# Convolutions taken from a queue of their own, first transposes in other PSUM banks, and norms placed elsewhere in a hybrid decoder layer

## The chip, the cores and the metric

The kernel runs on one core of a Trainium2 chip. The metric is the device time of one execution in microseconds (us). The core's engines are PE (TensorE, matrix products into PSUM), DVE (VectorE), ACT (ScalarE), POOL (GpSimd) and SP (SyncE, which here issues DMAs); each runs its own list of instructions in order and waits on semaphores for the others.

## The reference, cut to what matters

One layer is computed for 512 prompt tokens and 8 x 4 sample tokens, 544 in all, with 1024 channels, in fp32. An RMSNorm stands before and after each of three blocks:

```python
x = x + 0.5 * rmsnorm(swiglu(rmsnorm(x, n_ffn1_pre), ffn1_wg, ffn1_wu, ffn1_wd), n_ffn1_post)   # 1024 -> 2816 -> 1024
mix, new = mixer(rmsnorm(x, n_mix_pre), ...)
x = x + rmsnorm(mix, n_mix_post)
x = x + 0.5 * rmsnorm(swiglu(rmsnorm(x, n_ffn2_pre), ffn2_wg, ffn2_wu, ffn2_wd), n_ffn2_post)

def swiglu(x, wg, wu, wd):
    return (silu(x @ wg) * (x @ wu)) @ wd

def mixer(u, ...):
    rg_x, rg_g, z, xbc, dt_raw, g_rg, g_ssd = split(u @ w_in)          # 1024 -> 10272
    rg_xc = causal_conv(rg_x, rg_conv_w, rg_conv_b)                     # 4 taps along time
    h = rg_lru(rg_xc, ...)       # gates sigmoid(rg_xc @ wa + ba), sigmoid(rg_xc @ wx + bx), then a scan over time
    y_rg = h * gelu(rg_g)
    xs, Bs, Cs = split(silu(causal_conv(xbc, ssd_conv_w, ssd_conv_b)))
    y = ssd_scan(xs, softplus(dt_raw + bias), -exp(a_log), Bs, Cs, ...)  # 32 heads in 8 groups, chunks of 128 tokens
    y = (y + ssd_d * xs) * silu(z)
    y_ssd = y * rsqrt(mean over each group(y * y) + EPS) * ssd_norm_w
    m = sigmoid(g_rg) * (y_rg @ w_proj_rg) + sigmoid(g_ssd) * (y_ssd @ w_proj_ssd)
    return m @ w_out, new states
```

## The kernel before, in words

Activations lie with channels on the partitions and the 544 tokens along the free axis, in two halves of 272 (`HALF`). Weights come in blocks of up to 1024 x 128. ACT casts a block to a rounded part `wh` (L75), and DVE subtracts that from the block, which gives the rest `wl` (L79); `WRAW` = 2 raw loads and `WBLK` = 4 split blocks are held. Activations are split in the same way (`xh`, `xl`). A block's product is three passes for each of its eight 128 x 128 tiles, wh on xh, wh on xl and wl on xh, summed in PSUM: `gemm` (L285) for both halves of the tokens, `gemm_half` (L317) for one half, where `pair` puts two blocks side by side in one accumulator.

PSUM has three kinds of tile: `acc` (two of two banks each), `ps` (two of one bank), `py` (one of two banks).

PE's order is the order in which the code is written. The lists of the other engines are put in order by a scheduler, from dependencies and priorities (`urgent()` raises one; weight splits are lowered); edges without a semaphore ("NOSYNC") fix an order on one engine.

Beside the gemms runs background work, written as generators in the list `bg`: norms, transposes, the RG-LRU (`rg_steps`, eight channel tiles taken in pairs, r0 = 0, 2, 4, 6), dt (`dt_steps`), the convolutions of the SSD branch and its groups (`group_steps`). `ptick()` counts gemm matmuls; at each `pace`-th, `tick()` lets the first generator of the list go on to its next `yield`. `wait(n)` is n yields. What a generator writes to PE thus stands at a place counted in gemm matmuls.

The places that the change touches, in the order of the program:

- *Start.* x is transposed untouched (L565, `to_half`): x[0], x[1] and x2a give the first 272 tokens, eight chunks of 128 channels into eight banks of all three kinds. ACT makes xh (L570), DVE xl (L571, `evac_half`). Squares for the norm (L546) run beside; the norm's factor `fac` reaches the first products later (L606, `first_factors`). The first gemm's accumulator takes the place of the `acc` tile that holds chunks 0 and 5. The other 272 tokens are squared, scaled (`scaled`) and transposed in the background (`first_norm`).
- *First transposes of x itself.* `turn_steps` (L655, DVE copies L656) brings x into the transposed layout for the residual; a step is five transposes.
- *RG pair 6* is the last pair; its gates are matmuls into `py` (L937), a sigmoid after each (L939), two gates for each of two channel tiles.
- *SSD groups.* For each of 8 groups the main stream has units for B, C, x0, x1 (their products are evacuated into `cb`, L734 to L737, and the last columns into `cq`, L877), gates, and z. A convolution is a first tap on ACT (L863), three taps on DVE (L865), a tanh on ACT (L1009), and two products on DVE (L1010, L1011). Then `group_steps`: `A(c)` transposes B and x of chunk c (L1041, L1043), scales on DVE (L1046) and takes exponentials on ACT (L1048, L1062); `Bs(c)` is the chunk's products; s0 to s4 are the sample tokens'. `s2(p)` evacuates two state transposes with an ACT copy each (hT, L1168). In `bg` the four convolutions of a group stand as entries of their own ahead of its `group_steps`, each with a `wait(3)` behind it.
- *Norms between blocks.* `between(..., waits)` waits so many ticks before its sums, factors and transposes.
- *End.* `y_units` adds the last product pair of a half to y (L439) and squares it (L426); in the last half `turn.last` weighs y by the norm's weight (L1470), `turn_last` transposes it (L1474, L1558), `finish` sums squares over channels with matmuls into one column per 128 tokens (L1536, three sources, 18 matmuls), takes the factor (L236, L239, L240 to L243) and adds it to x (L1553).

Of the kernel before, what the change touches and what calls it, by code (L numbers as in the profile page):

```python
# [18 lines left out]
P = 128  # L19
D = 1024  # L20
KD = 8
# [13 lines left out]
class Weights:  # L35
# [30 lines left out]
    def _split_next(self):  # L66
# [26 lines left out]
WARM = 10  # L93

# [5 lines left out]
def hybrid_layer_kernel(  # L100
# [159 lines left out]
    pace = [8]  # L260
# [4 lines left out]

    def tick():
# [29 lines left out]
    def pair(kt, rh, rl, h, keep=None, key=None):  # L296
# [17 lines left out]
    def gemm_half(acc, j, wb, kt, rh, rl, h):  # L314
        for k in range(kt):
            for i, (w, r) in enumerate(((wb[0], rh), (wb[0], rl), (wb[1], rh))):
                PE.matmul(acc[:, j, :TH], w[:, k, :], r[k][:, HALF[h]],  # L317
                          start=(k == 0 and i == 0), stop=(k == kt - 1 and i == 2))
                ptick()
# [22 lines left out]
    def ffn(hid, open_pool, post, late=None, turn=None):  # L342
# [30 lines left out]
        for kind, i, h in ffn_order():  # L373
            if kind == "gu":
# [13 lines left out]
                else:  # L388
                    kept = keep if i == 1 else None
                    acc = pair(KD, xh, xl, h, kept, "g")  # L390
# [14 lines left out]
    def y_units(pool, tag, kt, rh, rl, n2, h, sqa, add, qscale, keep, turn=None):  # L405
# [6 lines left out]
        else:  # L412
            acc = pair(kt, rh, rl, h, keep if n2 in KEPT else None, n2)
            first, last = ((0, 3), (SECOND[0], SECOND[3]))[h]
            step = 1 if n2 == last else 2
            alone = turn is not None and n2 == last
            if alone:
                qv = turn.squares()
            else:
                q = pool.tile([P, T], F32, tag=tag, name="sq", bufs=6 if tag == "ld" else 2)  # L420
                qv = two(q)
            for j in range(0, 2, step):
                yv = yb[:, 2 * n2 + j:2 * n2 + j + step, HALF[h]]
                with urgent():
                    evac_y(yv, acc[:, j:j + step, :TH], add)
                    S.activation(qv[:, j:j + step], yv, AF.Square, scale=qscale)  # L426
                    if alone:
                        turn.last(j)
                    elif n2 == first:
                        V.tensor_add(sqa[:, HALF[h]], q[:, HALF[0]], q[:, HALF[1]])  # L430
                    else:
                        for i in range(j, j + step):
                            V.tensor_add(sqa[:, HALF[h]], sqa[:, HALF[h]], q[:, HALF[i]])
            if turn is not None and not alone:
                turn.pair(n2)

    def evac_y(y, acc, add):
        if add:
            V.tensor_add(y, y, acc)  # L439
        else:  # L440
            S.copy(y, acc)

# [92 lines left out]
    def factors(srcs, on_vector=()):  # L535
# [1065 lines left out]
```

## Time and profile before

| | |
|---|---|
| three runs | 1747.27, 1741.66, 1745.37 us, median 1745.37 |
| the profiled execution | 1746.04 us, span 1744.2 us (1.8 us lie around the span) |
| PE busy | 1692.1 us, 97% of the span |
| DVE, ACT, POOL busy | 1000.7, 739.6, 260.4 us |
| matmuls of the gemms in three passes, one of them (L285, wh on xh) | 2576, mean 292 ns with overlap |
| bytes | 206.21 MB in 205551 packets, mean 118 GB/s |

How to read it: the span is what the trace covers, from the first to the last recorded instruction; the profiled execution's own time lies 1.8 us above it. Matmuls overlap in the array, so the mean of 292 ns is longer than the pitch from one to the next. Busy times say what an engine did, not whether the end waited for it: for that one reads the waits.

### The profile page before, as it was taken

Reading aid. Unit: us, or ns where it says so; the run is one execution under the profiler, and the core shown is the slowest. Engines: PE = TensorE matmul, PEld = TensorE weight load, DVE = VectorE, ACT = ScalarE, POOL = GpSimd, SP = SyncE. Lnnn points to the kernel's source line nnn. Section 1 sums busy time; section 2 is a strip of 40 time slices with the busy share of each in tenths; the row PEclk is TensorE's granted clock in tenths of the full one; section 3 lists DMA queues with packets and bytes.
Section 4 is the critical chain, followed back from the end, with each engine's and each line's share of the span. In section 5 each row is a group of like instructions: output and inputs, shape, how many; then the busy total and the mean of one; then the engine's idle time right before and its main releaser. Section 6 shows DMA issues by size and latency. Waiting matters only on the chain. (4 is left out here: it accounts for less than half of the span.)

```text
span 1744.2 us, 32098 instructions
## 1 busy us (share of the span) xinstructions
PE 1692.1 (97%) x13485; PEld 1649.7 (95%) x13485; DVE 1000.7 (57%) x1764; ACT 739.6 (42%) x1204; POOL 260.4 (15%) x376
## 2 busy tenths in 40 slices
PE   8999999999999998999999999999999999999997
PEld 8899999999999997998988988999999999999997
DVE  5632333237757578788689687776558332233335
ACT  6323221234568674545545545434246423221233
POOL 0000000000222125345344333230000000000000
PEclk9999999999999998999999999999999999999999
DMA  6223232233543333524443535666324323223231
GB/s 208 84 75 114 74 98 84 87 97 109 164 156 112 101 97 107 165 88 113 146 144 93 157 114 155 214 189 221 137 80 139 115 68 109 85 85 97 75 120 52
DMA packets 205551, 206.21 MB, mean 118 GB/s; under 512 B 10461, under 2 KB 191785, under 8 KB 205150
## 3 DMA queue, kind: packets, MB, share of 16 engines
q1 hardware_dynamic: 196588, 178.49, 33.1%
q0 software_dynamic: 8336, 24.54, 4.3%
q8 instruction: 106, 1.74, 0.4%
q10 hardware_dynamic: 482, 1.12, 0.2%
q14 instruction: 39, 0.32, 0.1%
HBM read 178.43 MB, written 25.69 MB: 117 GB/s over the span
## 5 line engine op out<-in xcount | busy, mean ns | idle before, releaser
L75 ACT CAST wh<-wraw 128x1024 fp32r<-128x1024 f32 (+1 forms) x274 | 283.6, 1037 | 645.9 <-PE acc L285 535.0
L285 PE MATMUL acc<-xh,wh 128*128 128x272 f32 x2576 | 544.3, 292 | 0.1
L285 PE MATMUL acc<-xh,wl 128*128 128x272 f32 x2576 | 541.7, 292 | 0.0
L285 PE MATMUL acc<-xl,wh 128*128 128x272 f32 x2576 | 539.3, 291 | 0.0
L79 DVE TENSOR_TENSOR wl<-wraw,wh 128x1024 fp32r<-128x1024 f32 (+1 forms) x274 | 331.3, 1212 | 320.3 <-ACT wh L75 317.2
L285 PEld LDWEIGHTS acc<-xh,wh 128*128 128x128 f32 x2576 | 409.0, 190 | 3.5 <-issue 1.4
L285 PEld LDWEIGHTS acc<-xh,wl 128*128 128x128 f32 x2576 | 407.3, 190 | 2.6 <-issue 1.2
L285 PEld LDWEIGHTS acc<-xl,wh 128*128 128x128 f32 x2576 | 408.3, 190 | 1.2 <-issue 0.4
L317 PE MATMUL acc<-xh,wh 128*128 128x272 f32 x384 | 114.6, 298 | 3.3 <-DVE xl L571 3.3
L317 PE MATMUL acc<-xh,wl 128*128 128x272 f32 x384 | 113.8, 296 | 0.0
L317 PE MATMUL acc<-xl,wh 128*128 128x272 f32 x384 | 113.4, 295 | 0.0
L386 DVE TENSOR_TENSOR gate<-gate,acc 128x544 f32<-128x544 f32 x36 | 26.0, 721 | 132.0 <-PE acc L285 132.0
L865 DVE SCALAR_TENSOR_TENSOR cv<-cb,hp,cv 128x568 f32<-128x568 f32 x96 | 93.9, 978 | 1.1
L285 PE MATMUL acc<-hh,wh 128*128 128x272 f32 x448 | 92.5, 288 | 0.0
L285 PE MATMUL acc<-hl,wh 128*128 128x272 f32 x448 | 92.2, 287 | 0.0
L285 PE MATMUL acc<-hh,wl 128*128 128x272 f32 x448 | 92.2, 288 | 0.0
L1551 POOL TENSOR_TENSOR xtok<-xtok,yo 32x512 f32<-32x512 f32 x1 | 1.3, 1257 | 535.7 <-ACT yo L1550 535.7
L725 POOL MEMSET cb<- 128x3 f32 x40 | 4.1, 102 | 510.1 <-PE acc L317 434.7
L317 PEld LDWEIGHTS acc<-xh,wh 128*128 128x128 f32 x384 | 74.4, 194 | 3.9 <-DVE xl L571 3.4
L317 PE MATMUL acc<-hh,wh 128*128 128x272 f32 x256 | 75.0, 293 | 0.0
L317 PEld LDWEIGHTS acc<-xl,wh 128*128 128x128 f32 x384 | 74.4, 194 | 0.5
L317 PEld LDWEIGHTS acc<-xh,wl 128*128 128x128 f32 x384 | 74.2, 193 | 0.3
(397 smaller groups left out, 2642.5 us busy)
## 6 DMA issues: line engine op xcount, KB each, us to landing
wraw<-in_w_in_dram SPq DMA_DIRECT2D x34, 1024.0 KB, 5.6
wraw<-in_ffn_wu_dram SPq DMA_DIRECT2D x24, 1024.0 KB, 5.3
wraw<-in_ffn_wg_dram SPq DMA_DIRECT2D x23, 1024.0 KB, 5.2
wraw<-in_ffn_wd_dram SPq DMA_DIRECT2D x20, 1024.0 KB, 5.2
wraw<-in_w_in_dram SPq DMA_DIRECT2D x18, 512.0 KB, 4.3
big<-acs_dram SPq DMA_DIRECT2D x32, 256.0 KB, 5.6
big<-in_state_ssd_dram SPq DMA_DIRECT2D x32, 256.0 KB, 6.0
out_dram<-big POOLq DMA_DIRECT2D x32, 256.0 KB, 3.6
```

The lines of the kernel that those rows point to most:

```text
L75: c = nc.scalar.copy(h[:, :kt], src)
L79: nc.vector.tensor_sub(l[:, :kt], src, h[:, :kt].bitcast(F32))
L285: PE.matmul(acc[:, h, :TH], w[:, k, :], r[k][:, HALF[h]], start=(k == 0 and i == 0), stop=(k == kt - 1 and i == 2))
L317: PE.matmul(acc[:, j, :TH], w[:, k, :], r[k][:, HALF[h]], start=(k == 0 and i == 0), stop=(k == kt - 1 and i == 2))
L386: V.tensor_mul(two(gs[j]), two(gs[j]), acc[:, :, :TH])
L725: G.memset(buf[:, 0:3], 0.0)
L865: V.scalar_tensor_tensor(o[:, :CO], buf[:, k:k + CO], ws[k], o[:, :CO], op0=ALU.mult, op1=ALU.add)
L1551: G.tensor_add(x[:n, cs], x[:n, cs], o[:n])
```

## The change

What it does, in the order of the program:

1. The first transposes go to the banks in the order acc, acc, acc, acc, ps, ps, py, py (two chunks to a tile). The first gemm of all (`apart`) does its sixteen passes with wh first, then its eight with wl. The cast of block 0 now stands behind chunk 2's xh, that of blocks 1 to 3 behind the last chunk's. `factors` is divided: `squares` after the evacuations (x2a's square on ACT behind the last xh), `factors` for Ln and Exp.
2. `pace` starts at 6, not 8.
3. The convolutions of the SSD groups go to a list `convs`. `conv_next(g, limit)` takes one if it belongs to group g, fewer than `limit` of that group have been taken, and at least `APART` = 7 ticks have passed since the last. It is called in each tick of the *previous* group's steps (limit 2, from A(3) on 3, from Bs(2) on 4), for group 0 in the ticks of RG pair 6 (limit 2). What is left is taken at the start of the group itself, with `wait(3)` behind each.
4. `between` waits 12 for 10 ticks in FFN 1 (first half) and 13 for 11 between mixer and FFN 2.
5. In the last pair of each half, y's part j = 0 is evacuated, squared and summed as soon as its own 24 matmuls are done (`done`), not after both.
6. At the end j = 0's squares are added to `sqa` on DVE; its sums run ahead, and only the last part's squares (`ql`, three matmuls) are summed after the last product; the two are added on DVE.

The core of the diff:

```diff
-        if self.after is not None and 0 < self.n_blk < WBLK:
-            after = self.after if self.n_blk == 1 else self.after2
-            self.tc.add_manual_dep(c.ins, after.ins.name, NOSYNC, reason="the input comes first")
+        if self.n_blk < WBLK:
+            self.tc.add_manual_dep(c.ins, self.after[self.n_blk > 0].ins.name, NOSYNC, reason="the input comes first")
...
-    pace = [8]
+    pace = [6]
...
+    def conv_take():
+        g, work = convs.pop(0)
+        work()
+        convs_done[g] += 1
+        conv_at[0] = ticks[0]
+
+    def conv_next(g, limit):
+
+        if convs and convs[0][0] == g and convs_done[g] < limit and ticks[0] >= conv_at[0] + APART:
+            conv_take()
+
     def tick():
+        ticks[0] += 1
         while bg:
             try:
                 next(bg[0])
                 return
             except StopIteration:
                 bg.pop(0)
+        if convs:
+            conv_next(convs[0][0], 4)
```

The queue's two users (the generator of RG pair 6 and a group's steps; every other `wait` in the two became `steps` in the same way):

```diff
+        def steps(n):
+            for _ in range(n):
+                yield
+                if r0 == KD - 2:
+                    conv_next(0, 2)
+
...
-            yield from wait(4)
+            yield from steps(4)
...
     def group_steps(g, tiles):
+        while convs_done[g] < 4:
+            conv_take()
+            yield from wait(3)
         Bt, Ct, x0, x1, z0, z1 = (tiles[i] for i in range(6))
+        limit = [2]
+
+        def steps(n):
+            for _ in range(n):
+                yield
+                conv_next(g + 1, limit[0])
+
...
+        yield from steps(2)
         A(3)
-        yield from wait(3)
+        limit[0] = 3
+        yield from steps(3)
         yield from s3(0)
         Bs(2)
-        yield from wait(3)
+        limit[0] = 4
+        yield from steps(3)
         yield from s2(1)
         yield from s3(1)
         Bs(3)
...
-            bg.append(conv_steps(f, buf, out, i))
+            convs.append((g, lambda f=f, buf=buf, out=out, i=i: conv_ssd(f, buf, out, i)))
```

The start:

```diff
+    def squares(srcs, on_vector=(), after=()):
 
         m = len(srcs)
-        ssq, t, r = (pi.tile([P, m], F32, name=f"{n}{m}", tag=n, bufs=2) for n in ("ssq", "ssq_t", "ssq_r"))
+        ssq = pi.tile([P, m], F32, name=f"ssq{m}", tag="ssq", bufs=2)
...
+                if i in after:
+                    put_behind(a, W.after[1])
+        return xn, ssq
+
+    def factors(ssq):
+
+        t, r = (pi.tile(list(ssq.shape), F32, name=f"{n}{ssq.shape[1]}", tag=n, bufs=2) for n in ("ssq_t", "ssq_r"))
+        rstd_act(ssq, t, r, W.after[1])
+        return r
...
     first = ((xt[0], P), (xt[1], P), (x2a, 16))
-
-    a, b, t = acc_tile(), acc_tile(), py_tile()
-    banks = [a[:, 0], b[:, 0], ps_tile(), ps_tile(), t[:, 0], a[:, 1], b[:, 1], t[:, 1]]
+    banks = []
+    for t in (acc_tile(), acc_tile()):
+        banks += [t[:, 0, :], t[:, 1, :]]
+    banks += [ps_tile(), ps_tile()]
+    t = py_tile()
+    banks += [t[:, 0, :], t[:, 1, :]]
...
-    first_r = factors(first, (1,))[1]
-    turned = None
+    turned = []
     for k in range(KD):
-        a = evac_half(banks[k][:, :TH], 0, k)
-        if turned is not None:
-            tc.add_manual_dep(a.ins, turned.ins.name, NOSYNC, reason="in the order of their use")
-        turned = a
-        if k == 3:
-            W.after = a
-    W.after2 = turned
+        turned.append(evac_half(banks[k][:, :TH], 0, k))
+        if k:
+            put_behind(turned[k], turned[k - 1])
+    W.after = [turned[2], turned[-1]]
+    first_ssq = squares(first, (1,), (2,))[1]
```

Order of the passes, last pairs and end:

```diff
-            gemm_half(acc, j, wbs[j], kt, rh, rl, h)
+            gemm_half(acc, j, wbs[j], kt, rh, rl, h, apart and j == 0)
+            if done is not None:
+                done(acc, j)
...
+    def gemm_half(acc, j, wb, kt, rh, rl, h, apart=False):
+
+        passes = ((0, rh), (0, rl), (1, rh))
+        order = [(k, p) for k in range(kt) for p in passes]
+        if apart:
+            order = [(k, p) for k in range(kt) for p in passes[:2]] + [(k, passes[2]) for k in range(kt)]
+        for n, (k, (w, r)) in enumerate(order):
+            PE.matmul(acc[:, j, :TH], wb[w][:, k, :], r[k][:, HALF[h]], start=(n == 0), stop=(n == len(order) - 1))
+            ptick()
...
+            def out(acc, j, step=1):
                 yv = yb[:, 2 * n2 + j:2 * n2 + j + step, HALF[h]]
                 with urgent():
                     evac_y(yv, acc[:, j:j + step, :TH], add)
-                    S.activation(qv[:, j:j + step], yv, AF.Square, scale=qscale)
+                    S.activation(ql if alone and j else two(q)[:, j:j + step], yv[:, 0] if alone and j else yv,
+                                 AF.Square, scale=qscale)
                     if alone:
                         turn.last(j)
+                    if alone and j:
+                        pass
                     elif n2 == first:
                         V.tensor_add(sqa[:, HALF[h]], q[:, HALF[0]], q[:, HALF[1]])
                     else:
                         for i in range(j, j + step):
                             V.tensor_add(sqa[:, HALF[h]], sqa[:, HALF[h]], q[:, HALF[i]])
+
+            acc = pair(kt, rh, rl, h, keep if n2 in KEPT else None, n2, out if n2 == last else None)
+            if n2 != last:
+                out(acc, 0, 2)
             if turn is not None and not alone:
                 turn.pair(n2)
 
```

```diff
-        yield from between(f1.tmp, xT, sqa, R_F1POST, R_MPRE, h, table, ((4, 10, 1), (4, 8, 1))[h])
+        yield from between(f1.tmp, xT, sqa, R_F1POST, R_MPRE, h, table, ((4, 12, 1), (4, 8, 1))[h])
...
-            bg.append(between(tmp, xT, sqa, R_MPOST, R_F2PRE, h, table, ((1, 11, 0), (4, 8, 1))[h]))
+            bg.append(between(tmp, xT, sqa, R_MPOST, R_F2PRE, h, table, ((1, 13, 0), (4, 8, 1))[h]))
...
+        V.memset(v[:, :, :3], 1.0)
         turn_last(2 * SECOND[3], 0)
-        for i, t in enumerate(TAIL):
-            for m, (src, o) in enumerate(srcs(t)):
-                PE.matmul(v[:NT[t], 0, i:i + 1], src[:, o:o + NT[t]], ones_d[:, 0:1], start=(m == 0), stop=(m == 2))
-        turn_last(2 * SECOND[3] + 1, 1)
+        for m, src in enumerate((sqa[:, 2 * P:], turn.q)):
+            if m:
+                sm = f2.pool.tile([P, 3], F32, name="fm")
+                S.copy(sm, v[:, 0, :3])
+                turn_last(2 * SECOND[3] + 1, 1)
+            for i, t in enumerate(TAIL):
+                PE.matmul(v[:NT[t], m, i:i + 1], src[:, P * i:P * i + NT[t]], ones_d[:, 0:1], start=True, stop=True)
         ra, r = (f2.pool.tile([P, 3], F32, tag=n, name=n) for n in ("fa", "fr"))
         with urgent():
-            rstd_act(v[:, 0, :3], ra, r, table)
+            V.tensor_add(sm, sm, v[:, 1, :3])
+            rstd_act(sm, ra, r, table)
```

Where the change moves instructions, the lists of an engine show it (line, operation, result <- sources, shape; "x2" is two of it in a row). Line numbers of the changed kernel are higher. First ACT at the start, before; L570 is a chunk's xh, L546 a square, L75 a block's cast (the first one shown is block 1's):

```order
L570 ACTIVATE xh_101<-acc,w1T 128x272
L75 CAST wh<-wraw 128x1024
L570 ACTIVATE xh_102<-py,w1T 128x272
L546 ACTIVATE xn,ssq_378<-yb 128x1024 x2
L546 ACTIVATE xn,ssq_378<-xs_in 32x1024
L75 CAST wh<-wraw 128x1024
L236 ACTIVATE ssq_t_379<-ssq_378,eps_t 128x3
L75 CAST wh<-wraw 128x1024
```

and after, where L608 is xh, L578 a square, L237 and L240 Ln and Exp:

```order
L608 ACTIVATE xh_101<-py,w1T 128x272
L608 ACTIVATE xh_102<-py,w1T 128x272
L578 ACTIVATE xn,ssq_249<-x2a 16x1024
L578 ACTIVATE xn,ssq_356<-yb 128x1024
L237 ACTIVATE ssq_t_295<-ssq_249,eps_t 128x3
L578 ACTIVATE xn,ssq_356<-yb 128x1024
L240 ACTIVATE ssq_r_296<-ssq_t_295 128x3
L578 ACTIVATE xn,ssq_356<-xs_in 32x1024
L75 CAST wh<-wraw 128x1024
L237 ACTIVATE ssq_t_364<-ssq_356,eps_t 128x3
L75 CAST wh<-wraw 128x1024
```

Block 1's cast, which stood between chunks 6 and 7, now follows four squares, Ln and Exp; block 0's (not shown) stands behind chunk 2.

PE in the first products of FFN 1, before, where the second of the gate's products ends and its stream of background steps runs out (L317 a pass of the gemm, L655 a step of `turn_steps`):

```order
L317 MATMUL acc<-xh_102,wh 128x272
L317 MATMUL acc<-xl_110,wh 128x272
L317 MATMUL acc<-xh_102,wl 128x272
L655 MATMUL ps<-ident,yb 128x128 x4
L655 MATMUL ps<-ident,xs_in 128x32
L655 MATMUL ps<-ident,yb 128x128 x4
L655 MATMUL ps<-ident,xs_in 128x32
L655 MATMUL ps<-ident,yb 128x128 x4
L655 MATMUL ps<-ident,xs_in 128x32
```

and after, a little earlier in the stream (L344 the pass, L693 the step):

```order
L693 MATMUL ps<-ident,yb 128x128 x4
L693 MATMUL ps<-ident,xs_in 128x32
L344 MATMUL acc<-xh_97,wh 128x272
L344 MATMUL acc<-xl_105,wh 128x272
L344 MATMUL acc<-xh_97,wl 128x272
L344 MATMUL acc<-xh_98,wh 128x272
L344 MATMUL acc<-xl_106,wh 128x272
L344 MATMUL acc<-xh_98,wl 128x272
L693 MATMUL ps<-ident,yb 128x128 x4
L693 MATMUL ps<-ident,xs_in 128x32
```

Of eight steps five stood in a row after matmul 192; now each has six matmuls behind it.

ACT in the gates of RG pair 6, before (L939 a gate's sigmoid, L1009 the tanh of a convolution of group 0, L734 to L737 and L877 evacuations, L863 a convolution's first tap):

```order
L939 ACT_TABLE_LOAD
L939 ACTIVATE in<-py,pT 128x568
L1009 ACTIVATE cv<-cv 128x568
L939 ACTIVATE in<-py,pT 128x568
L734 COPY cb<-acc 128x272
L736 COPY cb<-acc 128x240
L737 COPY cb<-acc 128x8x4
L75 CAST wh<-wraw 128x1024
L877 COPY cq<-cb 128x27
L863 ACTIVATE cv<-cb,hp 128x568
L939 ACTIVATE in<-py,pT 128x568 x2
```

and after (L983 the sigmoid, L1053 the tanh):

```order
L1053 ACT_TABLE_LOAD
L1053 ACTIVATE cv<-cv 128x568
L983 ACT_TABLE_LOAD
L983 ACTIVATE in<-py,pT 128x568 x2
L772 COPY cb<-acc 128x272
L774 COPY cb<-acc 128x240
L775 COPY cb<-acc 128x8x4
L75 CAST wh<-wraw 128x1024
L915 COPY cq<-cb 128x27
L901 ACTIVATE cv<-cb,hp 128x568
L1053 ACTIVATE cv<-cv 128x568
L983 ACTIVATE in<-py,pT 128x568 x2
```

Conv 0's tanh moved from behind the first sigmoid to ahead of it, with a table load of its own; conv 1's tanh, which came after the pair's square roots, now stands ahead of the third sigmoid.

More of the change, by code (lines that the diff above doesn't have):

```diff
@@ L389, in ffn @@
                     kept = keep if i == 1 else None
-                    acc = pair(KD, xh, xl, h, kept, "g")
+                    acc = pair(KD, xh, xl, h, kept, "g", apart=late is not None and (i, h) == (0, 0))
                     g = silu(acc, late() if late and h == 0 else None)
@@ L546, in factors @@
                 a = S.activation(xn[i][:n], x[:n], AF.Square, scale=D ** -0.5, accum_out=ssq[:n, i:i + 1])
-                if W.after is not None:
-                    tc.add_manual_dep(a.ins, W.after2.ins.name, NOSYNC, reason="the first half comes first")
-        rstd_act(ssq, t, r, table)
-        return xn, r
+                if i in after:
[5 more added lines that the diff above has]
+        return r
     def scaled(srcs, engines):
-        xn, r = factors(srcs)
+        xn, ssq = squares(srcs, after=(0, 1, 2))
+        r = factors(ssq)
         for i, (x, n) in enumerate(srcs):
@@ L941, in rg_steps @@
                 lst.append(g)
-                yield from wait(4)
+                yield from steps(4)
             G.tensor_mul(gxs[j][:, :CO], gxs[j][:, :CO], xcs[j][:, :CO])
@@ L952, in rg_steps @@
             avs.append(av)
-        yield from wait(4)
+        yield from steps(4)
         ths = []
@@ L962, in rg_steps @@
             V.scalar_tensor_tensor(gx, t, 1.0, gx, op0=ALU.add, op1=ALU.mult)
-        yield from wait(4)
+        yield from steps(4)
         rc = slice(LP + 2, LP + 2 + 7 * NB - 6, 7)
@@ L968, in rg_steps @@
             V.tensor_mul(gxs[j][:, :CO], gxs[j][:, :CO], gas[j][:, :CO])
-        yield from wait(4)
+        yield from steps(4)
         for j, r in enumerate(rs):
@@ L985, in rg_steps @@
             ahead["z"] -= 1
-            yield from wait(4)
+            yield from steps(4)
     def rg_final():
@@ L1184, in s3 @@
                 V.tensor_copy(st8["yos"][:, p], yo[:, :P])
-            yield from wait(3)
+            yield from steps(3)
             for i in range(2):
@@ L1195, in s3 @@
                 dma(o_s_ssd[0, 4 * i:4 * i + 4, hs].rearrange("b h d n -> (h d) b n"), h0[i])
-                yield from wait(3)
+                yield from steps(3)
         def s4():
@@ L1241, in group_steps @@
         s4()
-        yield from wait(3)
+        yield from steps(3)
         ys = []
@@ L1258, in group_steps @@
         fin()
-        yield from wait(12)
+        yield from steps(12)
         v = py_tile()
@@ L1265, in group_steps @@
             last_tanh[0] = rstd_act(v[:, :, :TH], two(sqs[0]), two(r))
-        yield from wait(3)
+        yield from steps(3)
         for p in range(2):
@@ L1270, in group_steps @@
             dma(ys_dram[f], ys[p])
-        yield from wait(3)
+        yield from steps(3)
     last_tanh = [None]
```

59 lines of the change are left out of this document (25 added, 34 removed).

## The prediction

> **What bounds the kernel now.** I read the page first (engine totals), then the granted clock by window, then TensorE's waits, then timelines of the places where the diff reaches. On the page:
>
> ```profile
> PE 1692.1 (97%) x13485; PEld 1649.7 (95%) x13485; DVE 1000.7 (57%) x1764; ACT 739.6 (42%) x1204; POOL 260.4 (15%) x376
> ```
>
> TensorE is busy for 1692.1 of 1744.2 us, and the change removes only some tiny matmuls, so what it can win is idle time of TensorE and time at a lowered clock. The windows (columns: length, busy time of PE, PEld, DVE, ACT, POOL, granted clock, DMA share, GB/s) show where both are:
>
> ```profile
> core 0: us, PE busy (x) PEld busy (x) DVE busy (x) ACT busy (x) POOL busy (x), PEclk, DMA share, GB/s
> 10.00:20.00 10.00, 6.74 (x32) 6.44 (x32) 8.15 (x22) 9.36 (x19) 0.00 (x0) 0.66 0.81 265
> 50.00:60.00 10.00, 7.51 (x35) 6.10 (x36) 9.11 (x23) 3.04 (x7) 0.00 (x0) 0.69 0.00 1
> 620.00:630.00 10.00, 7.83 (x50) 7.61 (x49) 6.37 (x10) 4.87 (x10) 2.16 (x6) 0.83 0.16 59
> 630.00:640.00 10.00, 10.00 (x82) 10.00 (x81) 5.08 (x9) 8.19 (x14) 2.82 (x4) 1.00 0.21 55
> 660.00:670.00 10.00, 4.56 (x21) 4.37 (x21) 6.78 (x18) 2.97 (x6) 4.26 (x10) 0.57 0.64 197
> 676.00:1160.00 484.00, 466.03 (x3915) 440.41 (x3914) 390.12 (x791) 239.25 (x451) 189.74 (x253) 0.99 0.46 136
> ...
> 1345.00:1720.00 375.00, 374.26 (x2989) 373.26 (x2988) 136.33 (x172) 113.66 (x154) 0.00 (x0) 1.00 0.28 90
> ```
>
> Full speed is 82 matmuls in 10 us (630 to 640), 0.122 us each. From 10 to 20 and 50 to 60 only 32 and 35 were done, from 660 to 670 only 21. From 1345 to 1720 TensorE hardly idles: nothing to win there. Its largest waits by releaser (total, times, longest):
>
> ```profile
> PE ps L1041 <- ACT big L1168: 8.0, 5, 2.2
> PE ps L1043 <- DVE in L1010: 7.0, 2, 5.2
> PE ps L1165 <- ACT small L1059: 4.0, 3, 2.6
> PE acc L317 <- DVE xl L571: 3.3, 1, 3.3
> PE ps L655 <- DVE xT L656: 2.6, 4, 0.8
> ```
>
> **The start.** The first gemm waits for the bank of its accumulator, which a transpose also used:
>
> ```profile
> 10.51 0.23 PE L565 MATMUL py<-ident,x2a 16*128 16x16 f32 x1
> 14.00 0.60 PE L317 MATMUL acc<-xh,wh 128*128 128x272 f32 x1 [3.26 <-DVE xl L571]
> 22.67 0.93 PE L606 MATMUL ps<-dg,ones_d 128*128 128x128 f32 x6
> 9.39 0.29 ACT L236 ACTIVATE ssq_t<-ssq,eps_t 128x3 f32<-128x3 f32 x1
> 9.72 0.20 ACT L239 ACTIVATE ssq_r<-ssq_t 128x3 f32<-128x3 f32 x1
> 12.73 1.04 ACT L75 CAST wh<-wraw 128x1024 fp32r<-128x1024 f32 x1
> 14.05 1.06 ACT L546 ACTIVATE xn<-yb 128x1024 f32<-128x1024 f32 x1
> 13.46 0.90 DVE L571 SCALAR_TENSOR_TENSOR xl<-acc,w1T,xh 128x272 fp32r<-128x272 f32 x2
> 15.21 1.21 DVE L79 TENSOR_TENSOR wl<-wraw,wh 128x1024 fp32r<-128x1024 f32 x1
> ```
>
> With the new banks the first accumulator is freed by the first chunks, and the gemm can begin when the transposes end, 10.51 + 0.23, about 10.8. Its sixteen wh passes then go at the pace of DVE's xl (0.45 each, with one wl of 1.21 between): by these rows the last xl is ready near 13.4, the passes end near 13.7, and eight wl passes end near 14.7. But block 1 is now late. Before, its cast began at 12.73, ahead of all squares but the first two. After, the order on ACT puts x2a's square, three more squares (1.06 each), Ln and Exp (0.29, 0.20) ahead of it: xh ends near 12.2, plus 4 x 1.06 + 0.49 is about 16.9, cast to 17.9, wl to 19.2. So TensorE, idle from 14.7, gets two passes in near 18 and goes on at 19.2, most likely at a lowered clock again (0.66 in this window before). Gemm 48 with the L606 transposes ended at 22.67 + 0.93 = 23.6; I get 24.3: **+0.7**. Ends: -2.5 (the squares yield, only the first wait goes) and +2.5 (the lowered clock lasts on over another 3.4 us).
>
> **The first background transposes.** At pace 8 they end in a burst of five:
>
> ```profile
> L655 PE MATMUL ps<-ident,yb 128*128 128x128 f32 x20 | 4.0, 332 | 2.6 <-DVE xT L656 2.6
> ```
>
> The burst idles 2.6 us on DVE's copies out of two banks, and the clock falls: the mean of 0.69 from 50 to 60 is 6.2 us at half speed (2 x 0.31 x 10). Less about 0.8 of idle in it, half of that is lost: 2.7. At pace 6 the same steps stand six gemms (0.73 us) apart and all end before the pass does; DVE is not behind. **-5.3** (-2.6 if only the idle goes; -6.5). The Trainium skill (TensorE: Matmul & The Clock Gate, HAM oscillation) gives the rule "no PE-idle gaps >~3.4µs": single idles of 0.8 would then cost no clock, this term would be -2.6 and the sum 2.7 less. The clock of 0.69 in that row, with no idle longer than 0.8, is against it here.
>
> **The RG gates of pair 6.** There the new queue puts conv 0 and conv 1 of group 0 between the gates, and ACT's order changes: conv 0's tanh now stands ahead of sigmoid 1, conv 1's tanh ahead of sigmoid 3.
>
> ```profile
> 620.85 1.28 ACT L939 ACT_TABLE_LOAD   x1
> 624.62 0.73 ACT L939 ACTIVATE in<-py,pT 128x568 f32<-128x568 f32 x1 [2.48 <-PE py L937]
> 626.50 0.68 ACT L1009 ACTIVATE cv<-cv 128x568 f32<-128x568 f32 x1 [1.15 <-DVE cv L865]
> 634.25 0.73 ACT L939 ACTIVATE in<-py,pT 128x568 f32<-128x568 f32 x1 [1.78 <-PE py L937]
> 624.77 1.63 DVE L865 SCALAR_TENSOR_TENSOR cv<-cb,hp,cv 128x568 f32<-128x568 f32 x2
> 627.68 0.94 PE L937 MATMUL py<-big,small 128*128 128x284 f32 x6
> 665.77 0.69 PE L1043 MATMUL ps<-ident,in 128*128 128x128 f32 x2 [5.16 <-DVE in L1010]
> 650.53 0.67 DVE L1010 SCALAR_TENSOR_TENSOR in<-cv 128x512 f32<-128x512 f32 x1
> ```
>
> The tanh can't start before the convolution ends on DVE (624.77 + 1.63 = 626.4); it ends at 627.2, a second table load (1.28) follows, and sigmoid 1 ends at 629.2 instead of 625.35. It holds py, the one bank, so gate matmuls 2 wait from 627.7 to 629.3 (1.6). Conv 1's tanh comes at best near 636.4 (its evacuations, a cast and its first tap are queued behind sigmoid 2), so sigmoid 3 ends near 637.8 and gates 4 wait about 3.1. Sigmoid 4 ends near 639.6, not 634.98. The chain through Exp, Sqrt and scans to x1 thus starts some 5 us later, but the stretch of DVE between it and x1 has less in it: conv 1's output (650.53, 0.67 + 0.15) is done earlier, one wl and three scalings come after x1: about -1.5. TensorE arrives at x1's transposes 4.7 us plus some clock later, so its 5.16 there is mostly the same wait, taken earlier; x1, before at 665.77, comes near 669.4. **+3.6**, from 0 (the delay fits into the 5.16) to +6. The Trainium skill (ScalarE: Activation LUTs, What ACT_TABLE_LOAD costs) prices a switch at about 2.66 us with its drain; the trace's 1.28 ends where the next work can start, and by the page the term would be 1.4 larger, the sum -3.8.
>
> **The groups.** Up to twelve waiting ticks of the convolutions' own (three behind each of four, at four matmuls a tick) leave each group; four convolutions go into the ticks of the group before. A(0) to A(0) is then about 337 matmuls of the stream, not 372 (counted in the program), 4.3 us closer. From 676 to 1160 TensorE idled 484 - 466.0 = 18.0 us, and clock 0.99 adds about 5. Most of the idle is A's transposes waiting for the second hT copy (8.0) and L1165's wait (4.0). In groups 0, 1, 3, 5 the copy now stands behind a tanh, two exps, a cast and three evacuations:
>
> ```profile
> 751.67 0.58 ACT L1168 COPY big<-ps 128x512 f32<-128x512 f32 x1
> 752.30 0.49 PE L1041 MATMUL ps<-in 128*128 128x128 f32 x2 [1.37 <-ACT big L1168]
> ```
>
> Before, it ended at 752.25 behind cast, evacuations and cq; my walk through the new ACT rows puts it at 752.6 in the same frame. The start of a group, where A(0) waited behind its own convolutions, gets better, A(3) a little worse. **-1**; ends -8 (the waits shrink by half: 9 of idle and clock back, less 1) and +8 (rival below).
>
> **Second FFN and end.**
>
> ```profile
> 1333.78 1.18 PE L477 MATMUL ps<-ld,ones_d 128*128 128x272 f32 x4 [1.55 <-ACT ld L476]
> 1327.43 0.43 ACT L239 ACTIVATE rr<-ld 128x272 f32<-128x272 f32 x1
> 1732.08 0.91 DVE L1470 TENSOR_SCALAR yw<-yb,pT 128x256 f32<-128x256 f32 x4
> 1733.20 0.35 PE L1536 MATMUL acc<-ones_d,sqa 128*128 128x1 f32 x2
> 1734.99 0.26 ACT L236 ACTIVATE fa<-acc,eps_t 128x3 f32<-128x3 f32 x1 [2.36 <-PE acc L1536]
> ```
>
> Between mixer and FFN 2 the Exp (1327.43) stood behind a cast that waited for its weights; now it follows its Ln, so of 1.55 about 0.9 goes, and the last pair's half is evacuated 24 matmuls earlier (0.4): **-1.3** (0 to -2; two more ticks of 7 matmuls, 1.7 us, before the post norm are covered by the gemms between). The 12 for 10 in FFN 1 takes one wait of 0.4 away: **-0.4**. At the end, j = 0 is evacuated under the last 24 matmuls. Of the eighteen sums from 1733.20 to 1734.99 three are left after the last square, and a copy and an add (about 0.2) come in: Ln near 1733.5, **-1.5** (-0.5 to -2).
>
> **Sum.** 0.7 - 5.3 + 3.6 - 1 - 1.3 - 0.4 - 1.5 = -5.2. The profiled execution took 1746.04, 0.7 above the median of 1745.37, so 1740.8 on its own time and 1740.2 on the median's: I say 1740.5.
>
> **Rivals.**
> - *The squeeze costs nothing and the groups smooth out.* DVE's dense stretches (10.00 of 10 in places) are broken up, sigmoid 1's delay fits into the 5.16, and half of the groups' 18.0 + 5 us goes (-9). For it: the 5.16 is there to absorb. Against: the second hT copy is not on DVE. 1740.5 - 3.6 - 8 = 1729.
> - *A(3) becomes the bound: slower.* DVE's 390.12 of 484 is 81%; with eight groups 30 us closer it is 86%, and the hT copy has more ahead of it. Each of groups 0 to 6 then waits about 1.4 us longer (7 x 1.4 = 9.8), and those that reach 2 us draw the half clock as at 620 to 630 (0.83: 3.4 us at half, 1.7 lost), say three: 5. That is 1740.5 + 15 = 1755. It decides from a mean A(3) wait of about 1.6 + 1.4 = 3 us. For it: 1.37 and 2.2 are not far off the clock's step.
> - *The burst only moves.* The transposes draw the same wait at pace 6 and the first idle comes back behind block 1: 1740.5 + 5.3 = 1746, no change.
> - *Short idles cost no clock.* If the low clock from 50 to 60 has another cause than the burst's idles and stays, the burst gives 2.6: 1740.5 + 2.7 = 1743. Against: 0.69 and 0.83 stand just where TensorE idled. This is what the clock rule of the Trainium skill named above would give.
>
> **Chances.** Forecast 0.50 (1735 to 1746), smooth 0.20 (1728 to 1735), A(3) 0.18 (1748 to 1757), burst 0.07, clock rule 0.05. What a measurement can tell is 0.3%, 5.2 us: faster is below 1740.1, slower above 1750.6. The forecast's own half lies on each side of 1740: faster 0.20 + 0.26 + 0.01 = 0.47, slower 0.14 + 0.01 = 0.15, same 0.38. Range 1731 to 1752: it cuts the far parts of the smooth and the A(3) case, about 0.08 and 0.10.
>
> **What would show it.** Start: first gemm near 10.8, then a wait of 3 to 4 us for wh and wl of block 1. Burst: no L694 wait, clock 1.00 from 50 to 60. Pair 6: py matmuls of L983's gates waiting for ACT, 1 to 3 us, and x1 near 669 in before's frame. Groups: total of A's waits for L1221 near 8. End: three sums after the last square. I am wrong if the A(3) waits pass 3 us, if the clock in the groups falls to 0.97, or if the gates do not wait.

## The result, and the profile after

The changed kernel takes 1785.22 us (median of 4 runs, 1782.5 to 1788.6) against 1743.91 before (4 runs): ratio 1.0236, 95% interval 1.0209 to 1.0263. I had forecast 1740.5, with 1752 as the upper end: wrong in size and sign. The profiled execution took 1788.6, the slowest of the four, 3.4 above the median. The numbers below are of executions in the chip's usual state; one of the eleven of whole_evac took 5002.98 us and is not in its ratio.

On the page of the changed kernel, span and TensorE's line:

```profile
span 1786.9 us, 32107 instructions
PE 1706.1 (95%) x13479; PEld 1658.6 (93%) x13479; DVE 1005.2 (56%) x1766; ACT 743.7 (42%) x1206; POOL 265.3 (15%) x376
```

The span grew by 42.7. TensorE is busy 14.0 longer with six matmuls fewer, and idles 28.7 longer. Most of the 14.0 is matmuls at a lowered clock: the mean granted clock of the execution fell from 0.985 to 0.980, by which about 9.6 were lost (0.020 x 1786.9 - 0.015 x 1744.2, an estimate). Windows of the changed kernel, in the columns of before:

```profile
20.00:30.00 10.00, 8.83 (x45) 8.24 (x46) 6.81 (x14) 6.10 (x9) 0.00 (x0) 0.66 0.67 211
50.00:60.00 10.00, 10.00 (x75) 9.37 (x76) 8.00 (x21) 3.09 (x8) 0.00 (x0) 1.00 0.00 1
620.00:630.00 10.00, 6.61 (x39) 6.16 (x37) 7.88 (x13) 4.32 (x7) 2.39 (x6) 0.83 0.16 59
676.00:1160.00 484.00, 443.64 (x3658) 415.24 (x3658) 383.02 (x783) 235.40 (x450) 190.22 (x253) 0.97 0.43 128
```

From 50 to 60 the clock is 1.00 now: the burst is gone. From 676 to 1160, where the groups lie, TensorE was busy for 466.03 before and is for 443.64 now (the same stretch of time, with less of the work in it), and the clock fell from 0.99 to 0.97, one of the signs I had named for being wrong. The waits name a releaser that my prediction never spoke of:

```profile
PE ps L922 <- ACT cq L915: 24.8, 14, 3.5
PE ps L1094 <- DVE small L1197: 4.9, 4, 1.4
PE ps L1096 <- DVE in L1054: 4.7, 1, 4.7
PE py L981 <- ACT in L983: 3.8, 2, 2.7
PE ps L922 <- ACT small L1112: 2.6, 2, 1.3
PE ps L922 <- ACT cb L775: 2.4, 1, 2.4
PE acc L344 <- DVE yb L468: 2.4, 4, 0.8
PE acc L344 <- ACT wh L75: 2.2, 1, 2.2
PE acc L344 <- ACT yb L470: 1.3, 2, 0.8
PE acc L1594 <- DVE acc L1586: 0.9, 1, 0.9
```

L922 is `conv_state`: every second convolution also transposes the last columns of two channel tiles on TensorE, for the state output. In the kernel before, its counterpart (L884) is not among the waits at all, since a convolution's turn in `bg` came long after its products: in groups 1 to 7 these transposes started 23 to 80 us after the ACT copy of their columns (from the rows of L877 and L884). The queue takes the convolution while the products have only just been made: the second transpose of nearly every pair now starts 0.05 us after its copy. One of the fourteen, TensorE's two transposes first, then ACT's list at the same time:

```profile
687.01 0.27 PE L922 MATMUL ps<-ident,cq 128*27 128x128 f32 x1
690.20 0.41 PE L922 MATMUL ps<-ident,cq 128*27 128x128 f32 x1 [2.91 <-ACT cq L915]
686.75 0.68 ACT L1053 ACTIVATE cv<-cv 128x568 f32<-128x568 f32 x1 [1.97 <-DVE cv L903]
687.33 0.61 ACT L1101 ACTIVATE big<-big 128x512 f32<-128x512 f32 x1
687.85 0.61 ACT L1115 ACTIVATE big<-big 128x512 f32<-128x512 f32 x1
688.37 0.36 ACT L772 COPY cb<-acc 128x272 f32<-128x272 f32 x1
688.63 0.36 ACT L774 COPY cb<-acc 128x240 f32<-128x240 f32 x1
688.88 0.20 ACT L775 COPY cb<-acc 128x32 f32<-128x32 f32 x1
688.96 1.06 ACT L75 CAST wh<-wraw 128x1024 fp32r<-128x1024 f32 x1
689.91 0.23 ACT L915 COPY cq<-cb 128x27 f32<-128x27 f32 x1
```

The second tile's columns are copied last of all: behind a tanh, two exponentials, three evacuations and a weight cast. TensorE, which does its list in order, stands with every gemm behind it. The waits of A for the hT copy, 8.0 before, for which I had said "near 8", are not among the waits any more; as I read it, TensorE now comes late enough to find the copy done.

Where the time went, by the start of the n-th gemm matmul, counted from 0, in the two traces (after minus before, worked out from the rows of the passes):

| matmul | 48 | 300 | 3246 | 4440 | 4680 | 7290 | 8000 | 11500 | last |
|---|---|---|---|---|---|---|---|---|---|
| us | +4.7 | -0.8 | +0.9 | +0.9 | +5.3 | +48.8 | +40.7 | +42.0 | +43.4 |

At 7290 more of the groups' small matmuls lie behind than before, so a part comes back by 8000. Start and pace together gain 0.8, RG pair 6 loses 4.4, the groups about 35, the norms between blocks and the end about 4.

### The profile page after: what moved, and what is told of

The parts are those of the page before. It is cut to its first block, busy times and chain, and to the rows that moved or that the text cites. A ratio compares the mean times of both kernels' runs of the same rounds, so it can differ in the third digit from the quotient of the medians.

```text
span 1786.9 us, 32107 instructions
## 1 busy us (share of the span) xinstructions
PE 1706.1 (95%) x13479; PEld 1658.6 (93%) x13479; DVE 1005.2 (56%) x1766; ACT 743.7 (42%) x1206; POOL 265.3 (15%) x376
## 5 line engine op out<-in xcount | busy, mean ns | idle before, releaser
L75 ACT CAST wh<-wraw 128x1024 fp32r<-128x1024 f32 (+1 forms) x274 | 283.7, 1037 | 656.5 <-PE acc L306 548.6
L306 PEld LDWEIGHTS acc<-xh,wl 128*128 128x128 f32 x2576 | 410.1, 192 | 1.6 <-issue 0.4
L344 PE MATMUL acc<-xh,wh 128*128 128x272 f32 x384 | 116.0, 302 | 2.2 <-ACT wh L75 2.2
L344 PE MATMUL acc<-xl,wh 128*128 128x272 f32 x384 | 112.8, 294 | 0.0
L344 PE MATMUL acc<-xh,wl 128*128 128x272 f32 x384 | 111.5, 293 | 0.4 <-DVE wl L78 0.4
L306 PE MATMUL acc<-hl,wh 128*128 128x272 f32 x448 | 92.2, 287 | 0.0
L903 DVE SCALAR_TENSOR_TENSOR cv<-cb,hp,cv 128x568 f32<-128x568 f32 x96 | 88.0, 916 | 0.7
L344 PE MATMUL acc<-hh,wh 128*128 128x272 f32 x256 | 75.3, 294 | 2.4 <-DVE yb L468 2.4
L344 PEld LDWEIGHTS acc<-xh,wh 128*128 128x128 f32 x384 | 74.3, 193 | 3.5 <-ACT wh L75 2.4
L344 PEld LDWEIGHTS acc<-xl,wh 128*128 128x128 f32 x384 | 74.3, 194 | 0.3
L344 PE MATMUL acc<-hl,wh 128*128 128x272 f32 x256 | 74.3, 290 | 0.2
```

What stands on the lines that cost most here:

```text
L75: c = nc.scalar.copy(h[:, :kt], src)
L306: PE.matmul(acc[:, h, :TH], w[:, k, :], r[k][:, HALF[h]], start=(k == 0 and i == 0), stop=(k == kt - 1 and i == 2))
L344: PE.matmul(acc[:, j, :TH], wb[w][:, k, :], r[k][:, HALF[h]], start=(n == 0), stop=(n == len(order) - 1))
L903: V.scalar_tensor_tensor(o[:, :CO], buf[:, k:k + CO], ws[k], o[:, :CO], op0=ALU.mult, op1=ALU.add)
```

## The experiments

In each, "before" was run on the same chip (1743.6 to 1744.8). Medians are given; ratios are to before.

**state_later.** The transposes of the state wait until the group itself starts:

```diff
         if i % 2:
             df = (8, 1)[i // 2]
-            conv_state(o_p_ssd_conv, o_s_ssd_conv, [lasts.pop(0) for _ in range(2)], f - df, df)
+            qs = [lasts.pop(0) for _ in range(2)]
+            states.append(lambda: conv_state(o_p_ssd_conv, o_s_ssd_conv, qs, f - df, df))
...
             yield from wait(3)
+        for _ in range(2):
+            states.pop(0)()
+            yield from wait(1)
         Bt, Ct, x0, x1, z0, z1 = (tiles[i] for i in range(6))
```

> The changed kernel, but a convolution taken from the queue no longer issues the transposes of its last columns (conv_state) at once; they are issued at the start of the group that the convolution belongs to. Theory A: the loss is TensorE waiting in these transposes for the ACT copy of columns evacuated a moment before (24.8 + 2.6 + 2.4 = 29.8 us in the trace of after), and the clock that falls after such a wait (about 8 us more). Then about 36 us come back, 1785 to about 1749 (1744 to 1757), and those waits are gone. Theory B: the groups stand too close, ACT and VectorE are late anyway, and another wait takes the place: 1770 or more.

1766.06, ratio 1.0132 (1.0112 to 1.0152). 19.2 us came back, half of what theory A said: the waits named L922 are gone, but others stand there. Its waits (L1150 is a copy of the sample tokens' part, L1203 a product, L1227 the hT copy):

```profile
PE ps L1224 <- DVE small L1150: 7.2, 2, 3.6
PE ps L1100 <- DVE small L1203: 5.7, 5, 3.0
PE ps L1100 <- ACT big L1227: 4.0, 4, 1.5
PE ps L1240 <- ACT big L1227: 3.7, 2, 1.9
```

One of them in its timeline, VectorE's list, a row of POOL and then TensorE; L1057 and L1058 are the output of a convolution of the *next* group:

```profile
932.73 2.70 DVE L1212 TENSOR_SCALAR small<-small,toks 32x32 f32<-32x32 f32 x4
935.36 1.20 DVE L78 TENSOR_TENSOR wl<-wraw,wh 128x1024 fp32r<-128x1024 f32 x1
936.49 0.67 DVE L1057 SCALAR_TENSOR_TENSOR in<-cv 128x512 f32<-128x512 f32 x1
937.09 0.17 DVE L1058 SCALAR_TENSOR_TENSOR in<-cv 128x32 f32<-128x32 f32 x1
937.39 0.41 DVE L1150 COPY small<-ps 128x256 f32<-128x256 f32 x1
933.69 1.27 POOL L1111 TENSOR_TENSOR big<-big,small 128x512 f32<-128x512 f32 x1
937.85 0.66 PE L1224 MATMUL ps<-ident,big 128*128 128x128 f32 x4 [3.60 <-DVE small L1150]
```

The convolution's output is 0.8 of this. More comes from L1212: the first of its four products took 2.26, where most take 0.22, and ended as POOL's product ended; without that the wait would have been about 2.0 shorter (2.26 - 0.22, an estimate). The other wait of 3.6, at 1063.8, has the same in it. So both theories had a part, and the second one needed splitting.

**no_ahead.** The calls that take convolutions ahead do nothing:

```diff
-                    conv_next(0, 2)
+                    pass
...
-                conv_next(g + 1, limit[0])
+                pass
```

> The changed kernel, but no convolution is taken ahead of its own group (those of a group are all taken at its start, each with its three ticks, nearly as in the kernel before); everything else stays. Theory A and B alike: the queue carries all of the loss in the groups, so 1742 to 1748; by the times at equal matmul numbers the other parts lost 0.8 less at the first FFN's start, gained none there, and lost 1.7 + 1.3 + 0.7 later, so 1747 is my number. Rival C, that start, pace, evacuation by parts or end carry much of the 41 us: 1755 or more.

1748.53, ratio 1.0028 (1.0017 to 1.0039): as expected from A and B, against C. Taking convolutions ahead costs 36.7 us (1785.2 - 1748.5); all the other parts together cost about 5.

**rg_off.** Only `conv_next(0, 2)`, the call in RG pair 6, does nothing.

> The changed kernel, but the convolutions of group 0 are not taken in the ticks of RG pair 6. In the trace of after the way from matmul 4440 to 4680 took 4.4 us more than before, with gate matmuls waiting for a sigmoid (3.8). If that is a loss of its own, 1785 falls to about 1781 (1779 to 1782). If it is only the wait for x1 taken earlier, it stays at 1785 or rises, since group 0 then starts with two more convolutions of its own.

1781.22, ratio 1.0214 (1.0199 to 1.0229): 4.0 less. The waits of the gates for a sigmoid (3.8) are not in its trace. It is a loss of its own, though the two ratios' intervals just overlap: the trace of the changed kernel loses 4.4 at the same place.

**pace_only.** The kernel before with one number changed:

```diff
-    pace = [8]
+    pace = [6]
```

> The kernel before, with the first pace at 6 instead of 8 and nothing else. My prediction's step: the burst of transposes goes, -5.3, so 1744 falls to 1738.6 (-2.6 if only the idle goes and the clock stays low, 1741.3). If the burst only moves: 1744.

1737.57, ratio 0.9963 (0.9950 to 0.9976), a gain of 6.1 us. Its window:

```profile
50.00:60.00 10.00, 10.00 (x80) 9.92 (x79) 7.91 (x17) 5.33 (x11) 0.00 (x0) 1.00 0.01 2
```

Eighty matmuls at a clock of 1.00, where before there were 35 at 0.69. With the four idles of 0.5 to 0.8 the low clock is gone too, and more came back than the 2.6 of idle (5.2 in the two traces by matmul 300).

**conv_low.** state_later, and the convolutions of the queue at a lower scheduling priority:

```diff
         g, work = convs.pop(0)
-        work()
+        with tc.high_priority(offset=-LATER):
+            work()
```

> state_later with one more edit: the instructions of a convolution that is taken from the queue get a lower priority with the scheduler (by 90, as the weight splits have), so that on VectorE and ACT they stand behind more of the running group's own short steps. Theory B1: what is left of the loss in state_later (1766 against 1748 without taking ahead) is the running group's steps queued behind a convolution's taps and outputs (TensorE waited 7.2 us for a VectorE copy and 5.7 for a VectorE product there): 1757 or less. Theory B2: the groups' steps simply stand too close on TensorE and the engines' total work in that time is the limit, whatever its order: 1762 to 1770. The gates' share (4 us) stays in either case.

1763.72, ratio 1.0113 (1.0099 to 1.0127): 2.3 less than state_later, what B2 expected. The waits only changed their names (6.8 for the hT copy, 5.5 for x1's convolution). It did not settle the matter: a shift of 90 moved the outputs of the convolutions by 5 or 6 gemm matmuls in the median (worked out from the rows). TensorE idles 19.2 instead of 24.7 us in groups 1 to 6, but 8.3 instead of 4.6 in group 0, where x1's own convolution now comes late.

**late_take.** state_later, with the convolutions taken only in a group's last 18 ticks:

```diff
-        limit = [2]
+        limit = [0]
...
-        limit[0] = 3
...
-        limit[0] = 4
...
         fin()
+        limit[0] = 4
         yield from steps(12)
```

> state_later with one edit: the convolutions of the next group are taken only in the last 18 ticks of a group (after its last products, where it waits for its norm), not between its chunks; three of four fit there at 7 ticks' distance, the fourth stays at the group's start. Groups stand as close on TensorE as in state_later (A(0) to A(0) about 336 matmuls, counted in the program, against 332). Theory B1, convolutions in among the dependent steps of a running group delay them: most of the 12 to 14 us come back that state_later loses in the groups, 1750 to 1755 with the gates' 4 us still in. Theory B2, the closeness: 1762 to 1768.

1748.19, ratio 1.0019 (1.0010 to 1.0028): 17.9 us less than state_later, though A(0) to A(0) is about as short (347 matmuls on average, 340 in state_later, 372 before). That is against B2 and for B1, and more than I gave it. The waits in its groups, against the four rows of state_later (20.6 together):

```profile
PE ps L1100 <- ACT big L1227: 3.8, 4, 2.1
PE ps L1100 <- DVE small L1203: 2.9, 3, 1.3
PE ps L1224 <- ACT small L1118: 2.7, 4, 1.6
```

From A(0) of group 0 to 40 us after A(0) of group 7 TensorE idles 18.1 us, against 32.4 in state_later; 7.2 of the difference are the two waits for L1150, which are gone, as are the slow products of L1212.

But the convolutions do not run in the last 18 ticks. TensorE's list follows the order of the code; VectorE's and ACT's are put in order by the scheduler. For group 2, in gemm matmuls after A(0) of group 1 (worked out from the rows; the steps of group 1's chunks reach to 204):

| | outputs of its four convolutions, VectorE | transposes of its last columns, TensorE | its own A(0) |
|---|---|---|---|
| before | 78, 127, 158, 212 | 320, 344 | 376 |
| the change | 76, 96, 156, 206 | 76, 172 | 328 |
| state_later | 76, 111, 154, 206 | 308, 312 | 336 |
| late_take | 83, 127, 158, 206 | 320, 324 | 348 |

VectorE ran the convolutions among the chunks' steps before the change already, and does in late_take. What the queue moved by a long way is the transposes. From state_later to late_take an output moves by at most 36 matmuls in any group, but for one, behind some of the running group's steps. How much of the 17.9 is this order, and how much the slow products of L1212, no run here separates.

**late_now.** late_take with the transposes issued at once again, as the change has them (the edit of state_later undone).

> late_take, with the transposes of the last columns issued at once again, as in the change itself. If those transposes hurt in the change because the columns had been evacuated only a moment before, they cost little here, where a convolution is taken long after its unit: 1748 to 1753, and waits of the transposes for the ACT copy under 5 us. If they hurt wherever they stand in the stream: 1760 or more.

1756.96, ratio 1.0079 (1.0066 to 1.0093): outside what I expected, by 4 us. The transposes' wait for the columns is down to one:

```profile
PE ps L922 <- ACT cq L915: 0.8, 1, 0.8
```

Against the changed kernel this is one edit, the late takes, and it brings back 28.3 us: in the terms of the table, the transposes go with their convolutions to 248 and 308. Moving the transposes alone brought 19.2 (state_later) and both together 37.0, so the two edits remove in part the same waits.

With late takes it is not the columns that are late, and yet 8.8 us are lost against late_take. By equal matmul numbers they are lost at A(0) of group 0 (3) and between matmuls 5064 and 6864, where A(c) and L1218 wait longer (5.5 + 4.3 and 5.3). state_later also puts two ticks more ahead of each group's first transposes. Whether those ticks or the place of the transposes make the 8.8, no run here tells.

**cast_first.** no_ahead, with the second half's squares behind the cast of weight block 1:

```diff
                 if i in after:
-                    put_behind(a, W.after[1])
+                    put_behind(a, W.second if m == 3 and after == (0, 1, 2) else W.after[1])
```

> no_ahead (no convolutions ahead of their group), and the squares of the second half stand behind the cast of weight block 1 on ACT instead of ahead of it. In four traces with the new start matmul 24 began at 19.7 to 20.7 us whenever the first one began (11.1 to 13.7), so I hold block 1's cast, at 19.7 behind four squares, to set it. Then matmul 24 moves to about 17, and matmul 48 from 26 to 28 to about 24.5, as before the change: about 2.5 us less than no_ahead, 1746. If the low clock after the first transposes sets it: no change.

1742.15, ratio 0.9989 (0.9981 to 0.9998): 6.4 less than no_ahead, more than twice what I expected. The cast in the changed kernel, TensorE behind it, and the cast in cast_first:

```profile
19.66 1.03 ACT L75 CAST wh<-wraw 128x1024 fp32r<-128x1024 f32 x1
20.74 0.60 PE L344 MATMUL acc<-xh,wh 128*128 128x272 f32 x1 [2.22 <-ACT wh L75]
...
15.72 1.03 ACT L75 CAST wh<-wraw 128x1024 fp32r<-128x1024 f32 x1
```

In the traces, matmul 48 comes 4.0 us earlier than in no_ahead (22.25 against 26.30): TensorE no longer idles, and the low clock behind the idle goes too (0.50 for 3.4 us from 21.0 in no_ahead). The two profiled executions differ by 3.5 in all (spans 1746.8 and 1743.3), so the traces account for little more than half of the 6.4; the rest lies between executions.

**whole_evac.** no_ahead, with evacuation by parts for the very last pair alone:

```diff
-            acc = pair(kt, rh, rl, h, keep if n2 in KEPT else None, n2, out if n2 == last else None)
-            if n2 != last:
+            acc = pair(kt, rh, rl, h, keep if n2 in KEPT else None, n2, out if alone else None)
+            if not alone:
```

> no_ahead, but the last product pair of a half is evacuated when both parts are done, as before, except for the very last one. In the trace of after TensorE waited at the start of a pair's second part for the evacuation of the first (2.4 us for VectorE in four places, 1.3 for ACT in two). If that wait is new and not hidden, 2.3 to 3 us come back (the last pair keeps its 0.6): 1746. If the sums gain as much by coming earlier: 1748.5, no change.

1744.77, ratio 1.0007 (0.9998 to 1.0016): 3.8 less, where I expected 2.3 to 3; the two profiled executions differ by 1.5 only. The second part's first matmul writes the accumulator tile that the evacuation of the first part is reading, and waits for it, in six places, though the banks differ. Of the waits of 2.4 and 1.3 this is left:

```profile
PE acc L344 <- DVE yb L468: 0.3, 1, 0.3
```

**best_mix, best2, best3.** best_mix: no queue, pace 6, new banks with block 1's cast ahead, parts for the very last pair alone, and `V.memset` of the last accumulator made urgent. best2 is that with the norms' waits as before the change. best3 is late_take with the same edits, and without the calls in RG pair 6.

> What held up, together: the queue undone (convolutions as entries of their own again), pace 6, the new banks with the cast of block 1 ahead of the second half's squares, evacuation by parts for the very last pair alone, and the accumulator of the last sums cleared early (in the trace of after TensorE waited 0.9 us for that memset behind VectorE's last weighting). Against pace 6 alone (1737.6): the start within 1, the end 1.3 less, so 1736. If the start costs as in no_ahead: 1739.

1736.79, ratio 0.9958 (0.9944 to 0.9971).

> best_mix without the two longer waits of the norms between blocks (12 back to 10, 13 back to 11). In the trace of best_mix the way from matmul 8376 to 8510, where the second of these lies, took 1.9 us more than in pace_only. If the longer wait is what costs there, 1736.8 falls to about 1735 and the way at 8376 is as in pace_only; start 2.3 and end 1.2 better than pace_only then give 1734 to 1736. If not: 1736.8.

1735.40, ratio 0.9950 (0.9937 to 0.9964). It is 1.4 below best_mix, less than either run scatters (1734.7 to 1739.1, and 1735.0 to 1738.2); from matmul 8376 to 8510 the trace takes 21.8 as against 23.5, so the longer wait cost there, as expected.

> late_take with every other loss that the runs showed taken out: no convolutions in the ticks of RG pair 6 (4.0 in rg_off), block 1's cast ahead of the second half's squares (6.4 in cast_first), evacuation by parts for the last pair alone (3.8 in whole_evac), the last accumulator cleared early, the norms' waits as before the change. If these add, 1748.2 - 4.0 - 6.4 - 3.8 = 1734, less about 1.5 for the last two: 1732.5, some 3 below best2 (1735.4, without a queue), and the queue is worth something when it is taken where nothing waits. If it is worth nothing: 1735 to 1737, as best2.

1730.18, ratio 0.9924 (0.9910 to 0.9937), the best of all, 13.6 us below before and 2.3 below what I expected. On its page, and among its waits:

```profile
PE 1688.3 (98%) x13479; PEld 1645.8 (95%) x13479; DVE 992.2 (57%) x1763; ACT 738.3 (43%) x1198; POOL 267.6 (15%) x376
PE acc L308 <- ACT th L1361: 4.3, 1, 4.3
PE ps L1104 <- DVE in L1059: 4.0, 1, 4.0
```

The queue, with late takes and the transposes put off, is worth about 5 us against best2 (1735.4 to 1730.2; the intervals of the two ratios just meet, and the way from matmul 4440 to 8000 is 5.4 shorter in the trace). What remains in the rows are single waits: x1's convolution in group 0, which was there before (5.2), and a gate's tanh, for which TensorE had waited 0.4 before.

## Why the prediction was wrong, point by point

- *The step that failed is the groups, "-1".* I counted ticks and what stands ahead of the hT copy, and left out that a convolution issues TensorE work of its own, `conv_state`. It moved with the convolution, in group 2 by 172 to 244 gemm matmuls, to a place where its input is at the end of ACT's list: 24.8 + 2.6 + 2.4 us of waiting, and the clock that fell behind it. no_ahead measures the whole of taking ahead as 36.7 us with RG pair 6 (4.0) in it, so the term was about +33. Moving the transposes to the group's start brought back 19.2 (state_later), and writing the takes behind the running group's steps another 17.9 (late_take); the late takes alone brought 28.3 (late_now). What makes the part that the transposes do not explain stays open.
- *The slower rival had the sign, not the mechanism.* I gave 0.18 to groups so close that A(3) waits longer for hT. In the changed kernel A does not wait for it, and in state_later the waits for hT are 4.0 + 3.7, no more than the 8.0 before; the larger ones are for short VectorE steps. The closeness that I made its cause did little: late_take stands nearly as close as state_later and loses 17.9 less.
- *The start, +0.7*, was mis-sized. The mechanism, block 1's cast behind four squares, was right; the cast came at 19.66, not 16.9, and matmul 48 lost 4.7, beyond the +2.5 I gave as the end. Two things were missing: the transposes ran at 0.84 us a chunk in that execution (they had taken 0.53), and ACT waited 0.57, twice, for VectorE's xl of the chunk before, where two chunks share a PSUM tile. In late_take the transposes ran at 0.53 and block 1's cast still came at 18.50, so the slow transposes were the smaller part. cast_first returned 6.4, of which the traces show 3.5 to 4.
- *The burst, -5.3*, was right: 6.1 in pace_only, 5.2 in its trace by matmul 300. The rival by which short idles cost no clock (the burst giving 2.6) falls. The rule of the Trainium skill (TensorE: Matmul & The Clock Gate, HAM oscillation), idle above about 3.4 us, does not describe this trace: four idles of at most 0.8 did it.
- *RG pair 6, +3.6*, was right: 4.0 in rg_off. The gates wait 3.8 for the sigmoid that a tanh holds back. The parts were not as I had them: 2.7 at the second gate and 1.1 at the fourth, where I said 1.6 and 3.1.
- *FFN 1 and second FFN, -0.4 and -1.3*, had the wrong sign. I costed evacuation by parts as 24 matmuls earlier, at no price; TensorE waited for it at each pair's second part (2.4 + 1.3 us), and whole_evac returned 3.8. The wait of 0.4 in FFN 1 did go. The longer wait in front of FFN 2 was no help (best2): of the 1.55 there, 1.40 stayed, and another 0.46 came in.
- *The end, -1.5*: the way from the last gemm matmul to Ln shrank by 0.4 (3.94 to 3.55), that to the end of the span by 0.7 (13.18 to 12.43; with the same code as before it took 14.15 in pace_only, so this is within what executions differ by). In FFN 2 the waits for evacuation by parts (0.6 + 0.3) had cost more. Two rows of after say why the sums did not run ahead. VectorE clears their accumulator behind its last weighting, and TensorE waits:

```profile
1775.77 0.06 DVE L1586 MEMSET acc<- 128x6 f32 x1
1775.98 0.73 PE L1594 MATMUL acc<-ones_d,sqa 128*128 128x1 f32 x6 [0.90 <-DVE acc L1586]
```

The parts that no_ahead leaves in add up: 1743.9 - 6.1 (pace) + 6.4 (cast) + 3.8 (parts) = 1748.0, measured 1748.5. That is sums of separate runs, each uncertain by about 2, with the end and the norms' waits taken as nothing.

## What to carry to other kernels

Before moving a step earlier, list everything that it issues on each engine, and for each of these ask when its *input* is ready at the new place: transposes of 0.3 us on the engine that bounds the kernel waited 24.8 us in fourteen places, 0.4 to 3.5 each, because their operand was the last thing in another engine's queue. Where a scheduler orders an engine's list, the place where work is written is not the place where it runs: VectorE ran the convolutions among a group's chunks before and after the change (in group 2 at nearly the same matmuls), and what moved in full was the work on the engine that follows the written order. The same queue cost 37 us when it was filled from a group's first ticks on, and was worth about 5 when it was filled at the end of them and the transposes were put off. And an evacuation "by parts" is early only if the parts are separate tiles to whatever orders the waits.

## What the runs showed of the hardware that I had not expected

With the changed start the first gemm matmul began anywhere from 10.9 us (late_take) to 13.7 (the changed kernel) in profiles of identical code up to there, because the transposes ran at a full or at a lowered clock (chunks 0.53 or 0.84 us apart; the granted clock was 1.00 from 6.2 to 19.9 in late_take and 0.50 from 7.4 to 17.6 in no_ahead). Matmul 24 began at 19.6 to 20.7 in all of these, since a cast bounded it. In these runs the clock at the very start differed from execution to execution, and a step that rests on it needs more than one profile.

Four VectorE products of 32 x 32 took 2.70 us at 932.7 in state_later, against 0.67 for the same four at 869.7. The first of them alone took 2.26, and ended within 0.05 us of the end of POOL's product L1111; at 1058.7 the same happened again. At 869.7 POOL ran nothing. Whether POOL's work held them, no run here tests.
